# State-space decay factors: the mask by GpSimd, the column's decay as the exponential's bias

## The chip, the cores and the metric

The kernel runs on one core of one Trainium2 chip. The metric is the device time of one execution in microseconds. Before the change it is 2160.16 us, the median of three runs (2158.58 to 2160.63).

## The reference, cut to what matters

A sequence of 256 rows and 1024 columns passes four layers. Each layer is a SwiGLU block, a mixer and a second SwiGLU block, each followed by a layer norm. The mixers of layers 0 and 3 are state-space mixers; those of layers 1 and 2 are two kinds of attention. The part of the state-space mixer that the change touches is this:

```
a_cs     = cumsum(dt * a)                       # per head, along the 256 rows
decay_in = exp(where(l >= s, a_cs[l] - a_cs[s], -inf))
cb       = einsum('bclgn,bcsgn->bcgls', c, b)   # per group of eight heads
m        = cb * decay_in                        # per head, rows l, columns s
y_diag   = einsum('bcgrls,bcsgrp->bclgrp', m, xdt)
```

There are 32 heads in four groups of eight. A head's factor is zero above the diagonal, and it is multiplied by the group's `cb`.

## The kernel before

The 256 rows are two halves of 128, `t` = 0 and 1, which run as two interleaved streams on the same weights; the second follows the first by two pieces of weights (`LAG`). A piece is a tile `raw` of 128 x 2048 numbers. It is loaded by SyncE (SP), split by ScalarE (ACT) into a rounded part `wh` (L123) and by VectorE (DVE) into the rest `wl` (L124), four instructions each, and multiplied three times (L148 to L150: `wh` by `xh`, `wl` by `xh`, `wh` by `xl`). A scheduler orders the instructions of each engine from the program and its own estimate of durations. Each engine then works through its list strictly in order; so does each DMA queue.

In a state-space layer a group `g` goes through these stages in both streams:

- `stage_x` and `stage_bc` copy a finished projection out of its PSUM bank (L445, L453), transpose it on TensorE (PE) and put it in `xb`; `conv` (L423 to L434) runs on ACT and DVE, and the second stream's call does both halves.
- `stage_back` (L459) transposes back, makes `xdt`, `xD` and `xe` on DVE, multiplies b by c on PE (L478), and copies the result to `cb`. The first 128 columns are multiplied by the triangle mask on DVE (L481); the second stream's other 128 columns are copied by ACT (L483).
- `stage_m` (L496), twice per group and stream, makes the factors of four heads in a tile `mt` of 128 x 512. A DMA broadcasts four rows of running sums to all partitions (L500). DVE subtracts the column's sum and caps the difference at zero, one head at a time (L502). ACT takes the exponential of the whole tile (L503), and DVE multiplies it by `cb` (L504). The cap keeps the exponential finite above the diagonal, where the masked `cb` makes the product zero. Five buffers hold `mt`; each is free again when PE's last product with it is done.
- `stage_off` (second stream only) multiplies the carried state by `cb` on PE (L489), scales it (L491) and adds it (L494).
- `stage_y` multiplies each head's factor by `xdt` on PE (L512) and adds on DVE (L514); `stage_z` is the gate out of its PSUM bank (L519).
- `stage_n` multiplies by the gate (L524), squares on ACT (L526), scales the mean on DVE (L527), takes a power of -1/2 on GpSimd (POOL, L528) and scales the row by it on DVE (L529). `stage_a` transposes that on PE (L158) and splits it into `ah` and `al` for the output product.

So a layer has 16 tiles `mt` and eight of the powers. In these layers POOL otherwise does only small fills; its DMAs belong to the SwiGLU blocks.

Of the kernel before, what the change touches and what calls it, by code (L numbers as in the profile page):

```python
# [7 lines left out]
F32 = mybir.dt.float32  # L8
FR = mybir.dt.float32r
BF = mybir.dt.bfloat16  # L10
AF = mybir.ActivationFunctionType
ALU = mybir.AluOpType
# [11 lines left out]
NEG = -1e30  # L24
# [25 lines left out]
def build(tc, x, wst, ln_g, ln_b, sm_dt, sm_rows, sm_conv, sm_nw, fx_f, fx_b, out, plan=None):  # L50
    nc = tc.nc
    ctx = ExitStack()
    cpool = ctx.enter_context(tc.tile_pool(name="const", bufs=1))
# [13 lines left out]
    def T():  # L67
        return ps_t.tile([128, 512], F32, name="tp")
# [7 lines left out]
    def tmp(cols, tag, bufs, dt=F32):  # L76
        return spool.tile([128, cols], dt, name=tag, tag=tag, bufs=bufs)
# [6 lines left out]
    K = {}  # L84

    def consts():
        if K:
            return
        up = tmp(128, "t1", 5)
        make_upper_triangular(nc, up, val=1.0, diag=True)  # L90
        lo = tmp(128, "t1", 5)
        make_lower_triangular(nc, lo, val=1.0, diag=False)
        K["tri"] = cpool.tile([128, 128], FR, name="tri")
        nc.vector.tensor_copy(K["tri"], up)
        K["ntri"] = cpool.tile([128, 128], FR, name="ntri")
        nc.vector.tensor_scalar_mul(K["ntri"], up, -1.0)
        K["sel"] = cpool.tile([128, 32], FR, name="sel")
        nc.vector.tensor_add(K["sel"], ident[:, 0:32], ident[:, 32:64])
        K["strict"] = cpool.tile([128, 128], FR, name="strict")
        nc.vector.tensor_copy(K["strict"], lo)  # L100
        K["idb"] = cpool.tile([128, 128], BF, name="idb")
        nc.vector.tensor_copy(K["idb"], ident)
        K["mlo"] = cpool.tile([128, 128], BF, name="mlo")
        nc.vector.tensor_scalar_mul(K["mlo"], lo, NEG)
        K["mup"] = cpool.tile([128, 128], BF, name="mup")
        nc.vector.tensor_sub(up, up, ident)
        nc.vector.tensor_scalar_mul(K["mup"], up, NEG)
# [251 lines left out]
    def ssm_small(j):  # L359
        if j in ssms:  # L360
            return ssms[j]
        consts()
        s = St()
        s.dt = small_w(sm_dt[j], 32)
        s.rows = tmp(96, "rows", 1)
        nc.sync.dma_start(s.rows, bc(sm_rows[j:j + 1, :], 96))
        s.conv = spool.tile([128, 24, 5], F32, name="conv", bufs=1)
        nc.sync.dma_start(s.conv, sm_conv[j])
        s.na = tmp(32, "na", 1)
        nc.scalar.activation(s.na, s.rows[:, 32:64], AF.Exp)  # L370
        nc.vector.tensor_scalar_mul(s.na, s.na, -1.0)
        s.nw = {}
        s.xb, s.cv, s.B, s.xe = {}, {}, {}, {}
        ssms[j] = s
        return s
# [7 lines left out]
    def ssm(st, j):  # L383
        t = st.t
        s = ssm_small(j)
        d = St()
# [72 lines left out]
        def stage_back(g):  # L459
            cv = s.cv[g]  # L460
            h8 = slice(g * 8, g * 8 + 8)
            tp = T()
            for k in range(4):
                nc.tensor.transpose(tp[:, k * 128:(k + 1) * 128], cv[:, k, mine], ident)
            tp8 = tp.rearrange("p (a b) -> p a b", a=8)

            def times(tag, rows, bufs):
                o = tmp(512, tag, bufs)
                nc.vector.tensor_mul(o.rearrange("p (a b) -> p a b", a=8), tp8,
                                     rows[:, h8].unsqueeze(2).to_broadcast([128, 8, 64]))  # L470
                return o
            xds[g] = (times(f"xdt{t}", d.dt, 1 + t), times("xD", s.rows[:, 64:96], 2))
            if t == 0:
                s.xe[g] = times("xe", d.de, 1)
            tp = T()
            for n in range(1 + t):
                B = cv[:, 4, mine if n == 0 else slice(0, 128)]
                nc.tensor.matmul(tp[:, n * 128:(n + 1) * 128], B, cv[:, 5, mine], start=True, stop=True)  # L478
            cb = tmp(256, "t1", 5)
            nn = (1 + t) * 128  # L480
            nc.vector.tensor_mul(cb[:, :128], tp[:, :128], K["tri"].bitcast(F32))  # L481
            if t:
                nc.scalar.activation(cb[:, 128:], tp[:, 128:256], AF.Copy)  # L483
            cbs[g] = cb
            mts[g] = []

# [9 lines left out]
        def stage_m(g, qd):  # L496
            e = spool.tile([128, 4, 128], F32, name="mt", bufs=5)
            h0 = g * 8 + qd * 4
            row = d.cum[h0:h0 + 4, :].rearrange("h l -> (h l)").unsqueeze(0)
            nc.sync.dma_start(e.rearrange("p a b -> p (a b)"), row.to_broadcast([128, 512]))  # L500
            for h in range(4):
                nc.vector.tensor_scalar(e[:, h], e[:, h], d.ncum[:, h0 + h:h0 + h + 1], 0.0, op0=ALU.add, op1=ALU.min)  # L502
            nc.scalar.activation(e, e, AF.Exp)  # L503
            nc.vector.tensor_mul(e, e, cbs[g][:, 0:128].unsqueeze(1).to_broadcast([128, 4, 128]))  # L504
            mts[g].append(e)

# [37 lines left out]
        for g in range(N_GRP):  # L544
            b = where["X", g, 2]
            at(b - 1, stage_x, g)
            at(b, stage_bc, g)
            c = b + (LAG if t == 0 else 0)
            at(c + 1, stage_back, g)
            at(c + 2, stage_m, g, 0)  # L550
            at(c + 2, stage_m, g, 1)
            if t == 1:
                at(c + 2, stage_off, g)
            z = where["Z", g, 1]
            at(z, stage_z, g)
            iy = c + 3
            at(iy, stage_y, g)
            n = max(iy, z)
            at(n, stage_n, g)
            at(min(n + 1, where["O", g, 0] - 1), stage_a, g)  # L560
# [16 lines left out]
    def fox_small(j):  # L577
        if j in foxs:
            return foxs[j]
        consts()  # L580
        s = St()
        s.f = small_w(fx_f[j], 16)
        s.rows = tmp(16, "rows", 1)
        nc.sync.dma_start(s.rows, bc(fx_b[j:j + 1, :], 16))
        s.kT, s.v = {}, {}
        foxs[j] = s
        return s

    def attn(st, kind, j):
# [3 lines left out]
        if fox:  # L593
            s = fox_small(j)

            def stage_f():
                v = small_proj(st, s.f, 16, s.rows)
                q = log1p_exp(v, 16)
                m = small()
                nc.vector.tensor_scalar_min(m[:, :16], v, 0.0)  # L600
                lf = small()
                nc.vector.scalar_tensor_tensor(lf[:, :16], q[:, :16], -2.0, m[:, :16], op0=ALU.mult, op1=ALU.add)
                d.h, d.l = small_split(lf[:, :16])

            def stage_cum():
                d.rows = rows_T(d.h, d.l, K["ntri"], f"rowsT{t}")
                if t == 0:
                    s.toend = rows_T(d.h, d.l, K["strict"], "rowsTe")
        else:
            key = ("m", j)  # L610
            if key not in foxs:
                consts()
                foxs[key] = St()
                foxs[key].kT, foxs[key].v = {}, {}
            s = foxs[key]
# [315 lines left out]
```

## Time and profile before

| | us |
|---|---|
| median of three runs | 2160.16 |
| the profiled execution, whole | 2158.25 |
| its span | 2156.1 |
| PE busy | 2122.0 |
| DVE busy | 1486.4 |
| ACT busy | 1125.5 |

The granted TensorE clock is 0.999 of full speed over the span. The state-space layers lie at about 190 to 400 us and 1760 to 1970 us. An engine's busy share is counted over all stages, while the two state-space layers are a fifth of the span, so their own stretch has to be looked at. Instructions of one engine overlap by some tenths of a microsecond: a run of equal instructions takes less than their number times the mean of one.

### The profile page before, as it was taken

How to read it: one execution, taken by the hardware profiler on the slowest of the kernel's cores; microseconds unless marked ns; L12 is line 12 of the kernel's file. 1: busy time of each engine (PE TensorE's matmuls, PEld its weight loads, DVE VectorE, ACT ScalarE, POOL GpSimd, SP SyncE). 2: the span in 40 equal slices, each digit the busy share in tenths (PEclk: the TensorE clock that was granted, in tenths of full speed). 3: DMA queues.
4: the chain of work that ended last, by engine and by line, in shares of the span. 5: the costliest groups of instructions: out<-in, count | busy, mean ns of one | idle time of the engine just before them, and what ended most of it. 6: DMA issues, size and time to landing. Idle time of an engine off the chain costs nothing.

```text
span 2156.1 us, 29943 instructions
## 1 busy us (share of the span) xinstructions
PE 2122.0 (98%) x10370; PEld 1768.2 (82%) x10370; DVE 1486.4 (69%) x2959; ACT 1125.5 (52%) x2314; POOL 477.6 (22%) x862
## 2 busy tenths in 40 slices
PE   8999999999999999999999999999999999999998
PEld 6888878788888888888888888888888888788887
DVE  6657999855765674665575574666575679998655
ACT  6444776544444555444544455544454447665442
POOL 2331000233143200043233300033323310001431
PEclk9999999999999999999999999999999999999999
DMA  9775544676586643476666654376767665556772
GB/s 316 229 230 187 191 173 153 225 232 227 193 255 226 218 158 118 137 237 226 220 226 228 226 199 136 131 220 227 226 224 236 221 205 180 162 179 207 235 226 94
DMA packets 225927, 438.81 MB, mean 204 GB/s; under 512 B 20464, under 2 KB 20976, under 8 KB 225776
## 3 DMA queue, kind: packets, MB, share of 16 engines
q1 hardware_dynamic: 197616, 394.92, 55.1%
q0 software_dynamic: 28160, 41.99, 7.0%
q8 instruction: 81, 1.33, 0.3%
q14 instruction: 70, 0.57, 0.1%
HBM read 414.74 MB, written 22.09 MB: 203 GB/s over the span
## 4 chain that ended last, share of the span: by engine, by line
PE 93%; DVE 3%; ACT 1%; DMA 1%; issue 0%; POOL 0%; SPq 0%; DVEq 0%; ACTq 0%
PE gu L148 15%; PE gu L150 15%; PE gu L149 15%; PE acc L150 9%; PE acc L148 9%; PE acc L149 9%; PE ga L150 4%; PE ga L149 4%; PE ga L148 4%; PE tp L158 3%; PE gu L512 1%; DMA raw<-in_w_dram 1%; PE tp L657 1%; DVE wl L124 1%; DVE mt L502 1%
## 5 line engine op out<-in xcount | busy, mean ns | idle before, releaser
L124 DVE TENSOR_TENSOR wl<-raw,wh 128x512 fp32r<-128x512 f32 x1408 | 887.7, 683 | 361.8 <-ACT wh L123 360.2
L123 ACT ACTIVATE wh<-raw 128x512 fp32r<-128x512 f32 x1408 | 777.0, 621 | 528.0 <-PE gu L150 222.4
L148 PE MATMUL gu<-wh,xh 128*128 128x512 f32 (+1 forms) x1600 | 620.6, 388 | 7.1 <-ACT t L519 2.7
L150 PE MATMUL gu<-wh,xl 128*128 128x512 f32 (+1 forms) x1600 | 617.8, 387 | 0.9 <-DVE xl L124 0.9
L149 PE MATMUL gu<-wl,xh 128*128 128x512 f32 (+1 forms) x1600 | 617.4, 386 | 0.0
L246 POOL DMA_DIRECT2D aT<-turn x640 | 348.3, 551 | 503.4 <-issue 301.9
L148 PEld LDWEIGHTS gu<-wh,xh 128*128 128x128 f32 x1600 | 301.1, 188 | 69.7 <-ACT t L519 3.1
L150 PE MATMUL acc<-wh,al 128*128 128x512 f32 x896 | 353.5, 395 | 0.0
L149 PE MATMUL acc<-wl,ah 128*128 128x512 f32 x896 | 352.5, 393 | 0.0
L148 PE MATMUL acc<-wh,ah 128*128 128x512 f32 x896 | 351.5, 393 | 0.0
L150 PEld LDWEIGHTS gu<-wh,xl 128*128 128x128 f32 x1600 | 300.9, 188 | 61.6 <-DVE xl L124 2.1
L149 PEld LDWEIGHTS gu<-wl,xh 128*128 128x128 f32 x1600 | 301.2, 188 | 59.4 <-issue 0.5
L272 DVE TENSOR_TENSOR t<-t,gu 128x256 f32<-128x256 f32 x176 | 73.5, 418 | 192.5 <-ACT t L270 192.5
L270 ACT ACTIVATE t<-gu 128x256 f32<-128x256 f32 x176 | 67.5, 383 | 260.3 <-PE gu L150 239.5
L150 PEld LDWEIGHTS acc<-wh,al 128*128 128x128 f32 x896 | 168.4, 188 | 36.8 <-DVE al L124 1.9
L149 PEld LDWEIGHTS acc<-wl,ah 128*128 128x128 f32 x896 | 168.5, 188 | 34.4 <-issue 1.0
L148 PEld LDWEIGHTS acc<-wh,ah 128*128 128x128 f32 x896 | 168.5, 188 | 33.6
L148 PE MATMUL ga<-wh,xh 128*128 128x512 f32 (+1 forms) x448 | 159.6, 358 | 1.4 <-ACT xh L123 1.4
L242 POOL DMA_DIRECT2D turn<-tb x160 | 90.3, 565 | 318.6 <-DVE tb L240 297.7
L150 PE MATMUL ga<-wh,xl 128*128 128x512 f32 (+1 forms) x448 | 157.0, 351 | 0.1
L149 PE MATMUL ga<-wl,xh 128*128 128x512 f32 (+1 forms) x448 | 156.1, 349 | 0.0
L190 POOL TENSOR_TENSOR rstd<-ve,mhalf 128x1 f32<-128x1 f32 x24 | 22.6, 942 | 369.9 <-DVE ve L188 369.9
(179 smaller groups left out, 1707.0 us busy)
## 6 DMA issues: line engine op xcount, KB each, us to landing
raw<-in_w_dram SPq DMA_DIRECT2D x351, 1024.0 KB, 5.6
turn<-tb POOLq DMA_DIRECT2D x160, 128.0 KB, 3.4
aT<-turn POOLq DMA_DIRECT2D x640, 32.0 KB, 4.1
mt<-cums SPq DMA_DIRECT2D x32, 256.0 KB, 4.9
gb<-in_ln_g_dram SPq DMA_DIRECT2D x12, 512.0 KB, 4.6
gb<-in_ln_b_dram SPq DMA_DIRECT2D x12, 512.0 KB, 6.1
nw<-in_sm_nw_dram SPq DMA_DIRECT2D x8, 256.0 KB, 5.6
h<-in_x_dram SPq DMA_DIRECT2D x4, 256.0 KB, 4.3
```

Source lines behind the costliest of these rows:

```text
L123: a = nc.scalar.activation(wh, raw, AF.Copy)
L124: return a, nc.vector.tensor_sub(wl, raw, wh.bitcast(F32))
L148: nc.tensor.matmul(o, xh, wh, start=start, stop=False)
L149: nc.tensor.matmul(o, xh, wl, start=False, stop=False)
L150: nc.tensor.matmul(o, xl, wh, start=False, stop=stop)
L158: nc.tensor.transpose(tp[:, j * 128:(j + 1) * 128], src[:, j * 128:(j + 1) * 128], ident)
L190: nc.gpsimd.tensor_tensor(rstd, ve, mhalf, op=ALU.pow)
L242: nc.gpsimd.dma_start(dr, b.rearrange("p q k t -> p (q k t)"))
L246: nc.gpsimd.dma_start(aT[32 * q:32 * q + 32].rearrange("p i k t -> p i (k t)"), dv[q])
L270: nc.scalar.activation(sg, gu[:, :256], AF.Silu)
L272: nc.vector.tensor_mul(a, sg, gu[:, 256:])
L502: nc.vector.tensor_scalar(e[:, h], e[:, h], d.ncum[:, h0 + h:h0 + h + 1], 0.0, op0=ALU.add, op1=ALU.min)
```

## The change

`stage_back` now copies `cb` whole, 128 columns in the first stream and 256 in the second, on DVE and without the triangle. In `stage_m` a new instruction of POOL adds a mask of zero and -1e30 to the whole tile of four heads after its DMA; ACT then takes the exponential of one head at a time, with the negative of the column's sum as its bias, so that DVE's four subtractions are gone. Above the diagonal the exponential is now zero itself. A constant `mlf` holds the mask.

```diff
@@ consts
+        K["mlf"] = cpool.tile([128, 128], F32, name="mlf")
+        nc.vector.tensor_scalar_mul(K["mlf"], lo, NEG)
@@ stage_back
-            nc.vector.tensor_mul(cb[:, :128], tp[:, :128], K["tri"].bitcast(F32))
-            if t:
-                nc.scalar.activation(cb[:, 128:], tp[:, 128:256], AF.Copy)
+            nc.vector.tensor_copy(cb[:, :nn], tp[:, :nn])
@@ stage_m
             nc.sync.dma_start(e.rearrange("p a b -> p (a b)"), row.to_broadcast([128, 512]))
+            nc.gpsimd.tensor_tensor(e, e, K["mlf"].unsqueeze(1).to_broadcast([128, 4, 128]), op=ALU.add)
             for h in range(4):
-                nc.vector.tensor_scalar(e[:, h], e[:, h], d.ncum[:, h0 + h:h0 + h + 1], 0.0, op0=ALU.add, op1=ALU.min)
-            nc.scalar.activation(e, e, AF.Exp)
+                nc.scalar.activation(e[:, h], e[:, h], AF.Exp, bias=d.ncum[:, h0 + h:h0 + h + 1])
             nc.vector.tensor_mul(e, e, cbs[g][:, 0:128].unsqueeze(1).to_broadcast([128, 4, 128]))
```

The new kernel's lines are numbered a little differently: its addition is L501, its exponential L503, the power still L528, the fill of `xb` L445 (L443 before), `wh` L125 (L123), the copy out of the projection L447 (L445), the activation after the convolution L436 (L434).

On POOL, in the first state-space layer, the fills of `xb` and the powers (`sm` by `mhalf`) of the kernel before stand so:

```order
L443 MEMSET xb 128x6x3
L190 TENSOR_TENSOR rstd<-ve,mhalf 128x1
L443 MEMSET xb 128x6x3
L528 TENSOR_TENSOR sm<-sm,mhalf 128x1 x2
L443 MEMSET xb 128x6x3
L528 TENSOR_TENSOR sm<-sm,mhalf 128x1 x2
L443 MEMSET xb 128x6x3
L528 TENSOR_TENSOR sm<-sm,mhalf 128x1 x2
```

In the changed kernel the 16 additions to `mt` stand between them:

```order
L445 MEMSET xb 128x6x3
L192 TENSOR_TENSOR rstd<-ve,mhalf 128x1
L501 TENSOR_TENSOR mt<-mt,mlf 128x512 x2
L445 MEMSET xb 128x6x3
L501 TENSOR_TENSOR mt<-mt,mlf 128x512 x7
L528 TENSOR_TENSOR sm<-sm,mhalf 128x1 x2
L445 MEMSET xb 128x6x3
L501 TENSOR_TENSOR mt<-mt,mlf 128x512 x2
L528 TENSOR_TENSOR sm<-sm,mhalf 128x1
L501 TENSOR_TENSOR mt<-mt,mlf 128x512
L528 TENSOR_TENSOR sm<-sm,mhalf 128x1
L501 TENSOR_TENSOR mt<-mt,mlf 128x512
```

Nine additions now stand ahead of the first group's two powers. The ninth tile reuses the buffer of the first group's fourth.

On ACT, around the first group's factors in the first layer, the kernel before has one load of the exponential's table ahead of four exponentials (`mt`), between copies of weights (`wh`):

```order
L445 ACTIVATE t_2326<-ga 128x512
L434 ACT_TABLE_LOAD
L434 ACTIVATE cv<-cv 128x512
L123 ACTIVATE wh<-raw 128x512 x4
L483 ACTIVATE t_2280<-tp 128x128
L503 ACT_TABLE_LOAD
L503 ACTIVATE mt<-mt 128x512 x3
L123 ACTIVATE wh<-raw 128x512
L503 ACTIVATE mt<-mt 128x512
L519 ACT_TABLE_LOAD
L519 ACTIVATE t_2368<-ga 128x512
```

In the changed kernel single exponentials stand apart from the rest:

```order
L125 ACTIVATE wh<-raw 128x512 x4
L503 ACTIVATE mt<-mt,ncum 128x128
L436 ACT_TABLE_LOAD
L436 ACTIVATE cv<-cv 128x512
L503 ACT_TABLE_LOAD
L503 ACTIVATE mt<-mt,ncum 128x128 x6
L447 ACTIVATE t_2327<-ga 128x512
L503 ACTIVATE mt<-mt,ncum 128x128 x8
L519 ACT_TABLE_LOAD
L519 ACTIVATE t_2369<-ga 128x512
```

A single exponential ahead of the convolution's activation makes ACT load tables more often: the whole list has 52 loads where it had 40, and all twelve lie in the two state-space layers.

## Rows read from the trace of the kernel before

**Rows 1.** Busy time of each engine, share of the span, number of instructions.

```profile
PE 2122.0 (98%) x10370; PEld 1768.2 (82%) x10370; DVE 1486.4 (69%) x2959; ACT 1125.5 (52%) x2314; POOL 477.6 (22%) x862
```

**Rows 2.** Engine totals by stretch: SwiGLU blocks, then the first state-space layer.

```profile
core 0: us, PE busy (x) PEld busy (x) DVE busy (x) ACT busy (x) POOL busy (x), PEclk, DMA share, GB/s
450.00:620.00 170.00, 170.00 (x760) 140.46 (x759) 110.47 (x206) 81.45 (x169) 49.81 (x90) 1.00 0.68 222
200.00:370.00 170.00, 164.60 (x936) 139.74 (x936) 158.07 (x381) 115.67 (x210) 4.78 (x9) 1.00 0.54 183
```

**Rows 3.** What PE waited for: us in total, times, longest.

```profile
PE gu L489 <- ACT t L483: 2.9, 2, 1.4
PE gu L148 <- ACT t L519: 2.7, 2, 1.4
PE gu L512 <- DVE t L491: 2.1, 2, 1.0
```

**Rows 4.** DVE in order of time at the second group: start, duration, line.

```profile
278.82 3.22 DVE L502 TENSOR_SCALAR mt<-mt,ncum 128x128 f32<-128x128 f32 x16
281.96 2.49 DVE L504 TENSOR_TENSOR mt<-mt,t 128x512 f32<-128x512 f32 x4
```

**Rows 5.** ACT's groups by line and shape: busy us, mean ns.

```profile
L503 ACT ACTIVATE mt<-mt 128x512 f32<-128x512 f32 x32 | 19.5, 627 | 8.3 <-DVE mt L502 7.8
L503 ACT ACT_TABLE_LOAD x12 | 15.4, 1283 | 0.2
L667 ACT ACTIVATE mt<-tp,rs 128x128 f32<-128x128 f32 x32 | 11.3, 365 | 17.1 <-DVE rs L662 17.1
L483 ACT ACTIVATE t<-tp 128x128 f32<-128x128 f32 x8 | 2.2, 272 | 3.9 <-DVE t L481 3.9
```

**Rows 6.** POOL's groups by line: a fill and a select.

```profile
L618 POOL MEMSET qz<- 128x512 f32 x4 | 2.1, 527 | 154.2 <-PE tp L657 120.6 <-DVE t L514 33.6
masks.py:66 POOL TENSOR_SCALAR_AFFINE_SELECT t<-t 128x128 f32<-128x128 f32 x1 | 0.3, 305 | 0.0
```

**Rows 7.** In order of time: the first group's first power and its transposes.

```profile
252.41 0.68 DVE L524 TENSOR_TENSOR t<-t,t 128x512 f32<-128x512 f32 x1
252.58 0.93 POOL L528 TENSOR_TENSOR sm<-sm,mhalf 128x1 f32<-128x1 f32 x1 [18.12 <-DVE sm L527]
254.56 0.60 PE L158 MATMUL tp<-ident,t 128*128 128x128 f32 x4
```

**Rows 8.** The fourth `mt` DMA before that power, on SP's queue, and its landing.

```profile
L500 SPq DMA_DIRECT2D mt<-cums x1: 319/319/319, 248.7 to 248.7; - x1
...
DMA to landing us min/median/max: 4.0/4.0/4.0
```

**Rows 9.** The second group's second power.

```profile
295.79 0.42 DVE L124 TENSOR_TENSOR al<-tp,ah 128x256 fp32r<-128x256 f32 x1
295.95 0.55 POOL L528 TENSOR_TENSOR sm<-sm,mhalf 128x1 f32<-128x1 f32 x1 [2.74 <-DVE sm L527]
```

**Rows 10.** The two `mt` DMAs before that power, and their landing.

```profile
L500 SPq DMA_DIRECT2D mt<-cums x2: 319/320/320, 290.6 to 291.5; - x2
...
DMA to landing us min/median/max: 7.1/7.2/7.4
```

**Rows 11.** The third group's second power, in order of time.

```profile
344.19 0.55 POOL L528 TENSOR_TENSOR sm<-sm,mhalf 128x1 f32<-128x1 f32 x1 [4.70 <-DVE sm L527]
```

**Rows 12.** The `mt` DMA before that power, and its landing.

```profile
L500 SPq DMA_DIRECT2D mt<-cums x1: 319/319/319, 340.1 to 340.1; - x1
...
DMA to landing us min/median/max: 3.4/3.4/3.4
```

**Rows 13.** ACT in order of time ahead of a table load.

```profile
301.34 1.14 ACT L123 ACTIVATE wh<-raw 128x512 fp32r<-128x512 f32 x2
302.49 1.28 ACT L503 ACT_TABLE_LOAD   x1
```

## The prediction

> **What bounds the kernel now.** I read the page's totals first. PE is busy 98% of the span, DVE 69%, ACT 52% [rows 1], so a microsecond counts only where PE waits. The totals by stretch come next. Among the SwiGLU blocks PE has no idle time: 760 matmuls in 170 us, 0.224 us each. In the same length of a state-space layer PE is idle 5.4 us (170 less 164.60), DVE works 158.07 us and ACT 115.67 us [rows 2]. DVE is the engine closest to full there, with 12 us left; ACT has 54 us left and POOL 165. The table of PE's waits names what ends the idle time: the copy of `cb` on ACT, the gate's copy out of its bank on ACT, and the scaling of the carried state on DVE, each once in either layer, 1.0 to 1.4 us [rows 3]. So the change plays for about 5 us a layer on the good side. PE obeys its order, so new waits have no such limit.
>
> **The change part by part**, for one layer; there are two.
>
> *DVE loses work.* 64 subtractions go. Sixteen take 3.22 us [rows 4], 0.20 each in a run, so 12.9 us go. The copies of `cb` stay on DVE at about their old number and cost; I count nothing for them. The sixteen of the second group lie straight ahead of the scaling for which PE waits, with four multiplications behind them [rows 4]. Their place is taken by exponentials that ACT can do while DVE is still at the weights, so this wait of 1.0 us [rows 3] should go. I take -1.0. The copy for which the carried product waits (1.4 us) moves from ACT to DVE. It no longer has ACT's hop behind DVE's, but DVE gets to it at the same place in its list: -0.1.
>
> *POOL gains 16 additions of 128x512.* No row shows one. A fill of that shape, without an input, takes 0.53 us, and a select of 128x128, with one input, 0.30 us, four times which is 1.2 us [rows 6]. The lower end is 0.5; the upper end is twice 1.2, for two inputs, 2.4. I take 1.2, the row with an input. The Trainium skill ("GPSIMD Engine Reference", Elementwise — side-by-side cycle accounting) gives 2.6 cycles per element for a two-input addition, an estimate of 1.1 us for 512 elements before its fixed part.
>
> POOL has the time, so what counts is what stands behind an addition in its list. That is the power L528, on which the scaled row, the transposes and the output product hang. Before, the power waited only for DVE. Now the first group's powers stand behind the ninth addition, whose tile can only be fetched when PE has finished with the first group's last one. In the trace that fetch went out at 248.7 and landed 4.0 us later [rows 8]. 252.7 plus 1.2 is 253.9, and the power started at 252.58 [rows 7]: 1.3 us late. PE's order has 25 large matmuls and two small transposes between the group's last product and the transposes in either kernel, and PE came to those transposes without a wait (the row has no bracket) [rows 7]. So 1.3 us stand on PE. At the second group the second power stands behind one addition whose tile was fetched at 290.6 and landed after 7.1 us [rows 10]; 297.7 plus 1.2 is 298.9, against 295.95 [rows 9], 2.9 us late. Here the new order of PE has 16 large matmuls where the old one has 5, besides 24 half-size ones in both; eleven at 0.224 cover 2.5 us. 0.4 us remain. At the third group the fetch at 340.1, 3.4 us and 1.2 us make 344.7 [rows 12] against 344.19 [rows 11], 0.5 us late with one matmul more to cover it: 0.3. The fourth group's powers have no such addition ahead. Sum +2.0. With additions of 0.5 and 2.4 us this is +0.3 and about +5.
>
> *POOL and DVE get into each other's way.* A power of one column took 0.55 us where DVE was at an instruction with one input in PSUM [rows 9], and 0.93 us where DVE had just begun one with both inputs in SBUF, which ran till 253.09 [rows 7]. Something in the power waited for DVE; that an addition holds up DVE in turn, no row shows. If it does for its whole 1.2 us, and three DVE instructions in four have two SBUF inputs (`wl`, the convolution, the products), DVE loses 16 x 1.2 x 0.75 = 14.4 us, as much as it was given. The ends are a loss of 0 and of 29 us (2.4 each). I take the 14.4, since the reverse is seen: DVE's load stays at about 158 us, and nothing is given or taken on PE for it beyond the 1.1 above.
>
> The Trainium skill ("SBUF — State Buffer", Who interferes with whom) says so as a rule: DVE and GpSimd share a pair of ports, a DVE instruction with two SBUF inputs and a GpSimd instruction that reads SBUF exclude each other, and whichever comes second is blocked for the whole of the first. The two powers agree with it. By that rule the change moves DVE's work to a place where DVE pays for it again.
>
> *ACT gains work.* The nearest row to a one-head exponential with a bias is that of the attention's, 0.365 us [rows 5]. Instructions in a run overlap by 0.1 (two copies of weights take 1.14 [rows 13], where an exponential of the same shape shows 0.627 [rows 5]), so 0.27 in a run. 64 x 0.27 is 17.3 us; 16 whole-tile exponentials of 0.627 less 0.1 go, -8.4; six table loads of 1.283 come [rows 5], +7.7; four copies of 0.272 go, -1.1. ACT's list grows by 15.5 us to 131 of 170. The split weights, which are most of ACT's work, are named in none of PE's long waits [rows 3], so I take it that most of this is hidden by their being made ahead; without that cover all 15.5 us would stand on PE, which is the upper end, and 0 is the lower. On the path lie the copies out of PSUM banks that PE wants again: it waited 1.4 us a layer for the gate's [rows 3]. Of the six loads I let one (1.3 us) fall ahead of such a copy, with 0.2 for an exponential that waits for POOL: +1.5.
>
> The Trainium skill ("ScalarE: Activation LUTs", What ACT_TABLE_LOAD costs) counts about 1.38 us of drain with every load. In the trace the load starts 0.01 us after the copies ahead of it end [rows 13], so that no such time shows. By the page the term would be +2.9 and the sum 2.8 us higher over both layers.
>
> *The sum.* -1.0 - 0.1 + 2.0 + 1.5 = +2.4 us a layer, +4.8 in all. The profiled execution took 2158.25 us, 2.15 us more than its span, so 2163.0. The runs' median is 1.9 us above that execution, which would make it 2165. I say 2164.
>
> **The rivals.**
>
> *DVE's relief lasts (faster).* One mechanism: the additions don't hold DVE up, and DVE's 12.9 us let it run ahead of PE. Then the waits on DVE and on ACT behind DVE go, at most the 5.4 us a layer. For it: DVE has only 12 us left in the stretch, and the wait on L491 lies behind the removed work. Against it: the power's 0.93, and POOL's list. With two thirds of the idle time gone and 2 us of late powers hidden by the earlier start, -3.5 a layer: 2153. It decides if an addition costs DVE under 0.4 us.
>
> *The waits trade places (same).* The late powers and the vanished waits cancel, and ACT's loads hide in its 54 us. For it: all terms are 1 to 2 us. Time: 2160, within 3 us.
>
> *The port makes DVE the bound (slower by more).* By the port rule, as a mechanism here: additions of 2.4 us block DVE for 29 us a layer; 158 - 13 + 29 is 174 us in a stretch of 170. PE then waits for `wl`, 4 us a layer, and the late powers grow to 5 us, less the 1.0 that goes: +8 a layer, 2175. For it the two powers; against it that DVE instructions from PSUM can go on meanwhile, and that no row has an addition so long.
>
> **How the numbers follow.** No change can be told within 0.2%, 4.3 us. My forecast, slower by 1 to 11 us, has 0.46 (0.30 slower by over 0.2%, 0.16 within). DVE's relief has 0.24 (0.20 faster, 0.04 within), the trade 0.18 (0.13 within, 0.05 faster), the port as the bound 0.12 (all slower). That makes faster 0.25, same 0.33, slower 0.42. The range runs from 2152, just past the relief's 2153, to 2178, past the 2175 of the port; beyond it lie the longer tails of ACT's cost. The forecast's own range is 2159 to 2171.
>
> **What the changed profile would show.** If the steps are right: PE waits at the first group's transposes for DVE's L529, which waits for POOL, whose power starts right behind an addition; the wait of L512 on L491 is gone; POOL's additions take about 1.2 us; DVE instructions with two SBUF inputs are longer beside them; ACT has 52 table loads. The forecast is wrong if the power still waits for DVE alone, if DVE's instructions keep 0.68 us beside an addition, or if PE's waits in the layer fall under 3 us.

## The result, and the profile after

The changed kernel takes 2178.66 us (median of 5 runs, 2176.69 to 2179.07) against 2160.26 for the kernel before in the same session: a ratio of 1.0083 [1.0072, 1.0094], some 18 us slower. The profiled execution has a span of 2175.0 us against 2156.1, and its mean granted clock is 0.995 against 0.999.

The same stretch of the state-space layer, by its totals (span start, length, busy time and count of each engine, then the granted clock):

```profile
200.00:370.00 170.00, 158.58 (x878) 133.51 (x878) 147.57 (x300) 122.31 (x243) 29.20 (x25) 0.97 0.49 173
```

PE has done 878 matmuls where it had done 936 [rows 2]. DVE is busy for 147.57 us, less than the 158.07 of before: it is not full. The stretch also holds less of the layer now; for each matmul of PE, DVE is busy as long as before (0.168 us against 0.169). The clock, 1.00 before, is 0.97. So PE is late for things that DVE, with 22 us of idle time, makes too late.

What PE waited for over the whole program (us in total, times, longest), the answer to [rows 3]:

```profile
PE tp L160 <- DVE t L529: 7.3, 6, 2.6
...
PE tp L160 <- DVE t L455: 3.5, 1, 3.5
...
PE tp L403 <- ACT dah L125: 3.3, 2, 1.6
PE gu L150 <- DVE t L514: 2.2, 2, 1.1
...
PE gu L150 <- ACT t L519: 1.2, 2, 0.6
PE gu L512 <- DVE mt L504: 1.1, 1, 1.1
PE gu L512 <- DVE t L491: 0.9, 1, 0.9
...
PE gu L489 <- DVE t L483: 0.7, 2, 0.3
```

The three waits of [rows 3] have all shrunk: the copy of `cb` from 2.9 us to 0.7 (now on DVE), the gate's copy from 2.7 to 1.2, the scaling of the carried state from 2.1 to 0.9. Grown or new, among others, are the scaled row (L529), the copy of B and C out of their bank (L455), the step widths (`dah`) and the group's sum (L514). Three of the four are made by DVE, and the fourth by ACT, which had waited for DVE, as follows.

The first place in order of time (start, duration, engine, line; in brackets the idle time before it and what ended it):

```profile
221.03 2.86 POOL L501 TENSOR_TENSOR mt<-mt,mlf 128x512 f32<-128x512 f32 x2 [22.38 <-DMA mt<-cums]
221.07 1.29 DVE L316 TENSOR_SCALAR sm<-sm 128x32 f32<-128x32 f32 x1
...
222.67 1.28 DVE L318 SCALAR_TENSOR_TENSOR sm<-sm 128x32 f32<-128x32 f32 x1
...
224.27 0.18 DVE L318 SCALAR_TENSOR_TENSOR sm<-sm 128x32 f32<-128x32 f32 x1
...
224.88 0.63 ACT L436 ACTIVATE cv<-cv 128x512 f32<-128x512 f32 x1 [1.94 <-DVE cv L433]
...
229.22 0.29 ACT L125 ACTIVATE dah<-sm 128x128 fp32r<-128x128 f32 x1
229.57 0.33 PE L403 MATMUL tp<-tri,dah 128*128 128x128 f32 x1 [1.63 <-ACT dah L125]
```

Two additions run on POOL. Beside each of them one small DVE instruction takes 1.29 or 1.28 us, which takes 0.18 when nothing runs on POOL (the row at 224.27; L316 has a mean of 0.177 in e1, without additions). DVE loses 2.2 us; ACT waits 1.94 of them for the convolution; its list, in which `dah` stands further on, is late by as much; PE waits 1.63.

The costliest place is in the second layer:

```profile
1827.95 2.99 POOL L501 TENSOR_TENSOR mt<-mt,mlf 128x512 f32<-128x512 f32 x2 [2.44 <-DVE xD L494]
1828.39 6.47 DVE L126 TENSOR_TENSOR wl<-raw,wh 128x512 fp32r<-128x512 f32 x4
1831.22 3.08 POOL L501 TENSOR_TENSOR mt<-mt,mlf 128x512 f32<-128x512 f32 x2 [0.28 <-DMA mt<-cums]
...
1835.38 0.41 DVE L455 COPY t<-ga 128x256 f32<-128x256 f32 x1
1835.85 0.69 PE L160 MATMUL tp<-ident,t 128*128 128x128 f32 x2 [3.48 <-DVE t L455]
...
1836.76 0.63 PE L151 MATMUL ga<-wl,xh 128*128 128x512 f32 x1
1837.19 0.63 PE L152 MATMUL ga<-wh,xl 128*128 128x512 f32 x1
...
1842.08 0.39 PE L150 MATMUL ga<-wh,xh 128*128 128x512 f32 x1
1842.31 0.39 PE L151 MATMUL ga<-wl,xh 128*128 128x512 f32 x1
```

Four additions meet four weight splits, which take 6.47 us; three of them take 1.88 where POOL does nothing (the row at 285.00 of e5, below), so four some 2.5. The copy of the bank, behind them in DVE's list, comes 4 us late and PE stands for 3.48. When it goes on, its large matmuls start 0.43 us apart (1836.76, 1837.19) where they later start 0.23 apart. The granted clock of these stretches is the column before the last two:

```profile
1830.00:1835.00 5.00, 2.37 (x11) 1.63 (x9) 5.00 (x4) 1.65 (x4) 4.02 (x3) 1.00 0.22 65
1835.00:1840.00 5.00, 4.15 (x11) 3.38 (x12) 4.38 (x10) 3.02 (x6) 0.93 (x1) 0.50 0.60 211
1840.00:1845.00 5.00, 5.00 (x25) 4.19 (x25) 3.85 (x9) 3.90 (x9) 0.93 (x1) 0.82 0.16 61
```

After a stretch in which PE worked 2.37 of 5 us, the granted clock is 0.50, the 1.2 GHz level, and it is back at 2.4 GHz within the next 5 us. The same follows the wait at 229.57 (0.66 from 230 to 235). It does not follow every such wait: behind those of 1.63 us at 1808.49 and of 2.59 us at 1935.64 the granted clock stays at 1.00. By the mean clock the slow stretches hold at most some 9 us (0.005 of 2175 less 0.001 of 2156). PE's busy time says nearly the same: for the same 10370 matmuls it is 7.0 us longer than before (2129.0 against 2122.0). The other 11.9 us of the longer span are time in which PE stands.

### The profile page after: what moved, and what is told of

Read it like the earlier page. It is cut to its first block, busy times and chain, and to the rows that moved or that the text cites. A ratio compares the mean times of both kernels' runs of the same rounds, so it can differ in the third digit from the quotient of the medians.

```text
span 2175.0 us, 30015 instructions
## 1 busy us (share of the span) xinstructions
PE 2129.0 (98%) x10370; PEld 1772.0 (81%) x10370; DVE 1487.1 (68%) x2832; ACT 1158.0 (53%) x2414; POOL 527.9 (24%) x894
## 5 line engine op out<-in xcount | busy, mean ns | idle before, releaser
L126 DVE TENSOR_TENSOR wl<-raw,wh 128x512 fp32r<-128x512 f32 x1408 | 898.0, 690 | 369.5 <-ACT wh L125 367.6
L125 ACT ACTIVATE wh<-raw 128x512 fp32r<-128x512 f32 x1408 | 776.5, 621 | 520.9 <-PE gu L152 227.4
```

What stands on the lines that cost most here:

```text
L125: a = nc.scalar.activation(wh, raw, AF.Copy)
L126: return a, nc.vector.tensor_sub(wl, raw, wh.bitcast(F32))
```

## The experiments

Theory P was that the additions on POOL cost the time, theory A that ACT's short exponentials and table loads do. Theories B, C and Q then ask what it is about the additions: that they hold DVE up, that the chain through them is late, or that the powers behind them are. Theories L and O ask whether lost DVE time costs the same wherever it is lost.

| kernel | median us | ratio to before | DVE busy us | clock |
|---|---|---|---|---|
| before | 2159 to 2160 | 1 | 1486.4 | 0.999 |
| changed | 2178.66 | 1.0083 [1.0072, 1.0094] | 1487.1 | 0.995 |
| e1 no additions | 2146.35 | 0.9939 [0.9927, 0.9952] | 1462.6 | 0.999 |
| e2 additions alone | 2187.04 | 1.0134 [1.0118, 1.0149] | 1514.8 | 0.995 |
| e3 additions on DVE | 2150.67 | 0.9960 [0.9947, 0.9972] | 1481.6 | 0.999 |
| e4 `cb` whole alone | 2160.81 | 1.0008 [0.9999, 1.0017] | 1487.3 | 0.998 |
| e5 additions beside | 2170.21 | 1.0048 [1.0031, 1.0065] | 1481.7 | 0.992 |
| e6 fills beside | 2147.32 | 0.9943 [0.9928, 0.9958] | 1465.1 | 0.999 |
| e7 powers earlier | 2183.55 | 1.0106 [1.0091, 1.0121] | 1489.2 | 0.994 |
| e8 select on POOL | 2155.42 | 0.9982 [0.9973, 0.9991] | 1471.3 | 0.998 |
| e9 two additions on DVE | 2170.80 | 1.0057 [1.0044, 1.0069] | 1500.2 | 0.993 |
| e10 clamp on ACT | 2150.51 | 0.9960 [0.9946, 0.9973] | 1462.8 | 0.999 |
| e11 `dah` on DVE | 2176.28 | 1.0078 [1.0064, 1.0092] | 1486.9 | 0.993 |

**e1, the changed kernel without the additions.**

```diff
-            nc.gpsimd.tensor_tensor(e, e, K["mlf"]..., op=ALU.add)
...
-            nc.vector.tensor_scalar_mul(d.ncum, ps[:, :32], -1.0)
+            nc.vector.tensor_scalar_mul(d.ncum, ps[:, :32], 1.0)
```

> The changed kernel without its 32 additions on POOL (the triangle mask is left out and the bias of the exponential has its other sign, so that every factor stays finite: the decay factors are not the reference's). The exponentials by head, the whole copy of cb and the DVE without subtractions stay. Theory P (the additions cost the time: they hold up DVE's instructions, and the powers and exponentials stand behind them): no addition, so 2152 to 2162 us, and the waits of PE on L529 and L527 go back to the 0.9 us a layer of before. Theory A (ACT costs the time: 64 short exponentials a layer and their table loads come ahead of copies that PE waits for): the time stays at 2170 to 2180, the wait on the dah copy and the slow clock behind it stay.

2146.35 us: faster than before by 12.6. Theory A falls. ACT has the same 64 short exponentials and table loads a layer as the changed kernel, and of PE's waits in the first layer only three are left (us in total, times, longest):

```profile
PE gu L150 <- ACT t L518: 0.6, 1, 0.6
PE tp L160 <- DVE t L528: 0.5, 2, 0.4
PE gu L489 <- DVE t L483: 0.3, 1, 0.3
```

The rest of the change is a gain, then, and the 32 additions cost 32.3 us, one microsecond each (31.0 if the two kernels before, 2160.26 and 2158.99, are set equal). The time came out below the range of theory P too: I had not expected the relief to be worth so much.

**e2, the kernel before with the additions put in.**

```diff
+            nc.gpsimd.tensor_tensor(e, e, K["mlf"]..., op=ALU.add)
             for h in range(4):
                 nc.vector.tensor_scalar(e[:, h], e[:, h], d.ncum[...], 0.0, op0=ALU.add, op1=ALU.min)
```

> The kernel before, with the 32 additions of the mask on POOL put in ahead of its subtractions; the subtractions, the whole-tile exponentials and the masked cb stay. Theory P: all of the additions' cost and none of the relief, so 2174 to 2190 us, with powers behind additions. Theory A: the additions are hidden by POOL's free time, 2158 to 2166, and PE's waits are those of before.

2187.04 us, 28 more than before, as theory P has it. The waits are those of the changed kernel (same columns), though ACT works as before, and the three of [rows 3] are there too (2.9, 2.8 and 2.1 us):

```profile
PE tp L160 <- DVE t L532: 7.1, 7, 3.2
PE tp L160 <- DVE t L455: 3.9, 2, 2.0
...
PE tp L403 <- ACT dah L125: 3.7, 2, 1.9
```

**e3, the additions on DVE.**

```diff
-            nc.gpsimd.tensor_tensor(e, e, K["mlf"]..., op=ALU.add)
+            nc.vector.tensor_tensor(e, e, K["mlf"]..., op=ALU.add)
```

> The changed kernel with its 32 additions on DVE in place of POOL. DVE then pays about 0.7 us for each, nearly what the four subtractions took (0.8). Theory P: POOL's queue and the hold-up of DVE are gone, so 2156 to 2166 us. Theory A: ACT has the same exponentials and table loads as in the changed kernel, so 2172 to 2182.

2150.67 us, better than either theory's range and than both kernels. DVE does the 32 additions at 0.69 us each (19.0 us more busy time than in e1) for 4.3 us. Of POOL, nearly idle here, and DVE, nearly full, DVE was the better place.

**e4, `cb` copied whole, alone.**

```diff
-            nc.vector.tensor_mul(cb[:, :128], tp[:, :128], K["tri"].bitcast(F32))
-            if t:
-                nc.scalar.activation(cb[:, 128:], tp[:, 128:256], AF.Copy)
+            nc.vector.tensor_copy(cb[:, :nn], tp[:, :nn])
```

> The kernel before with cb copied whole by DVE (the triangle mask is left out, so the products above the diagonal are not the reference's) and nothing else changed. Both theories: PE's wait for the copy on ACT (1.4 us a layer) shrinks to under 0.5; the time is 2157 to 2161 us.

2160.81 us, no change that can be told. The wait did not shrink to 0.5: PE waits 1.3 us for the copy on DVE (line 481 there) where it had waited 1.4 for ACT's. DVE gets to it no earlier, which is what the prediction said of this edit (-0.1).

**e5, additions on POOL that nobody waits for.**

```diff
-            nc.gpsimd.tensor_tensor(e, e, K["mlf"]..., op=ALU.add)
+            junk = spool.tile([128, 4, 120], F32, name="junk", bufs=1)
+            nc.gpsimd.tensor_tensor(junk, cbs[g][:, 0:120]..., K["ntri"]..., op=ALU.add)
```

> The changed kernel without its additions on the tiles mt (mask left out, bias of the other sign: the decay factors are not the reference's), with 32 additions of 128x480 on POOL at the same places of the program that read cb and a constant and write a scratch tile that nobody reads. No exponential waits for them. Theory B (an addition blocks a DVE instruction for about a microsecond, whoever uses its result): most of the 32 us between the changed kernel and the one without additions comes back, 2166 to 2178 us, and DVE's instructions with their inputs in SBUF are longer beside the additions. Theory C (the chain fetch, addition, exponential, product is what is late): 2146 to 2152 us, since nothing of it stands in that chain.

2170.21 us: 23.9 of the 32.3 us come back with additions whose result is not used, and no instruction waits for them in the trace, so theory B holds. The 8.4 us left are no measure of theory C, since these additions also take DVE less time (19.1 us in place of 24.5) and start at other moments. Its chain shows little in the changed kernel: DVE stands for 1.8 us in all for the exponentials (2.1 before), and PE for 1.1 for `mt`. The largest wait of the first layer in order of time:

```profile
275.84 4.47 POOL L500 TENSOR_TENSOR junk<-t,ntri 128x480 f32<-128x480 f32 x3
...
276.24 4.63 DVE L124 TENSOR_TENSOR wl<-raw,wh 128x512 fp32r<-128x512 f32 x3
280.79 2.48 DVE L503 TENSOR_TENSOR mt<-mt,t 128x512 f32<-128x512 f32 x4
283.20 0.68 DVE L489 TENSOR_TENSOR t<-gu,ec 128x512 f32<-128x512 f32 x1
...
283.93 3.67 PE L511 MATMUL gu<-xdt,mt 128*128 128x64 f32 x16 [2.32 <-DVE t L489]
...
285.00 1.88 DVE L124 TENSOR_TENSOR wl<-raw,wh 128x512 fp32r<-128x512 f32 x3
```

Three splits take 4.63 us beside three additions, and 1.88 when POOL is done. The 2.7 us lost there are the 2.32 for which PE waits. The waits are the smaller part of the cost: over the whole program PE stands 9.0 us longer than in e1, and is busy 17.0 us longer with the same matmuls. Behind this wait the granted clock is 0.50:

```profile
285.00:290.00 5.00, 5.00 (x19) 4.49 (x19) 2.57 (x5) 0.00 (x0) 0.00 (x0) 0.50 0.40 130
```

**e6, fills in place of those additions.**

```diff
+            nc.vector.tensor_copy(junk[:, 0, 0:1], cbs[g][:, 0:1])
+            for _ in range(3):
+                nc.gpsimd.memset(junk, 0.0)
```

> As the run with the additions beside, but with three fills of 128x480 on POOL in place of each addition (about 1.5 us of POOL, no input read; a copy of one column on DVE ties them to the place). Theory B, if it is POOL's reading that holds DVE up: 2146 to 2154 us and DVE's instructions at 0.68. Theory Q (what stands in POOL's list ahead of the powers is late, whatever it does): as with additions beside, 2160 to 2175 us.

2147.32 us, 1.0 above e1. POOL is as busy as in e5 (525.6 and 526.6 us), and DVE's products of two SBUF tiles keep their time (mean ns behind the comma; 954 in the changed kernel):

```profile
L525 DVE TENSOR_TENSOR t<-t,t 128x512 f32<-128x512 f32 x16 | 10.9, 684 | 0.0
```

What holds DVE up is POOL's reading of SBUF, not its being busy. The Trainium skill says so ("SBUF — State Buffer", Who interferes with whom: a DVE instruction with two SBUF inputs contends with a GpSimd instruction that reads SBUF and not with one that only writes it); e5 and e6 agree.

**e7, the powers earlier in POOL's list.**

```diff
+            with tc.high_priority():
                 nc.vector.tensor_mul(y1, y1, th)
...
                 nc.gpsimd.tensor_tensor(ss[:, 2:3], ss[:, 1:2], mhalf, op=ALU.pow)
                 nc.vector.scalar_tensor_tensor(y1, y1, ss[:, 2:3], nw, op0=ALU.mult, op1=ALU.mult)
```

> The changed kernel with the normalisation chain (product, squares, power, scaling) scheduled at high priority, so that most powers stand one to three additions earlier in POOL's list; the additions stay. Theory Q: PE's waits on L529 (4.5 us in the first layer) go, 2164 to 2171 us. Theory B: the additions still block DVE, 2172 to 2182 us.

2183.55 us, no gain. But the edit did little of what it was meant to: in the trace only two of a layer's eight powers stand earlier in POOL's list, by one addition each, and the order of the other engines moved as well. The waits on the scaled row come to 6.7 us (7.3 in the changed kernel) with one of 3.3. So this run says little about theory Q. e5 says more: its waits on the scaled row are 1.0 us, as in e1, and its 23.9 us are there all the same.

**e8, a select with one input on POOL.**

```diff
-            nc.gpsimd.tensor_tensor(e, e, K["mlf"]..., op=ALU.add)
+            nc.gpsimd.affine_select(out=e, in_=e, compare_op=ALU.is_ge, fill=NEG, base=0, pattern=[[0, 4], [1, 128]], channel_multiplier=-1)
```

> The changed kernel with each addition on POOL replaced by a select of 128x512 with one input (it keeps the triangle and fills the rest with the mask's value; the mask tile is not read). Four selects of 128x128 took 1.2 us in the trace of before, so POOL's time is that of the additions. If two inputs on POOL are what blocks DVE: 2150 to 2160 us. If one is enough: 2172 to 2184 us, as the changed kernel.

2155.42 us. The number fits the first answer and the trace does not. I had taken the select to be as long as an addition, and its shortest takes 0.63, an addition's 1.27; beside it DVE is held up all the same, for a shorter time:

```profile
221.42 1.55 POOL L501 TENSOR_SCALAR_AFFINE_SELECT mt<-mt 128x512 f32<-128x512 f32 x2 [22.39 <-DMA mt<-cums]
221.45 0.64 DVE L316 TENSOR_SCALAR sm<-sm 128x32 f32<-128x32 f32 x1
...
222.41 0.61 DVE L318 SCALAR_TENSOR_TENSOR sm<-sm 128x32 f32<-128x32 f32 x1
```

0.64 in place of 1.29 for the same instruction L316. DVE's busy time is 8.7 us above e1's, and the time 9.1. One input on POOL is enough, and DVE is held up for as long as POOL's instruction takes (0.64 beside 0.63, 1.29 beside 1.27).

**e9, two additions on DVE.**

```diff
-            nc.gpsimd.tensor_tensor(e, e, K["mlf"]..., op=ALU.add)
+            nc.vector.tensor_tensor(e, e, K["mlf"]..., op=ALU.add)
+            nc.vector.tensor_tensor(e, e, K["mlf"]..., op=ALU.add)
```

> The changed kernel with each addition on POOL replaced by two on DVE (the mask is added twice; a factor above the diagonal is 0 either way). DVE then spends 2 x 0.69 us on each tile, 44 us in all, more than the about 25 us that the additions on POOL took from it. Theory L (what DVE loses is what counts, wherever it is lost): more than the changed kernel, 2176 to 2195 us. Theory O (the loss costs so much because POOL's additions stop DVE out of its order, in front of instructions that others wait for, while DVE's own additions stand where its list has room): one addition cost 4.3 us over none, so two cost 8 to 12: 2154 to 2160 us.

2170.80 us, between the two theories, and neither holds as it stands. The first 19.0 us of DVE's work cost 4.3 us, the next 18.6 cost 20.1: theory O's straight line is wrong. DVE is busy for 160.66 us of the stretch of 170 here; that its free time is used up is a likely reason, which no run tests alone. Nor is all of it waiting: of the 22.7 us between the spans of e9 and e3, 11.0 are PE's longer busy time. But with 13 us more of busy DVE than the changed kernel this one is 8 us faster, so theory L's equal price is wrong too. The clock fell here as well (0.993 over the span, 0.52 in the 5 us from 400, where PE had waited 2.03 us), with no addition on POOL.

**e10, the clamp on ACT.**

```diff
             for h in range(4):
-                nc.scalar.activation(e[:, h], e[:, h], AF.Exp, bias=d.ncum[...])
+                nc.scalar.activation(e[:, h], e[:, h], AF.Relu, scale=-1.0, bias=d.ncum[...])
+            nc.scalar.activation(e, e, AF.Exp, scale=-1.0)
```

> A version without the mask's addition: the clamp goes to ACT as a Relu by head with scale -1 and the column's decay as its bias, the exponential takes the whole tile with scale -1, and cb keeps its triangle by the product on DVE, with its second half copied by DVE too. No subtractions and no additions on DVE or POOL; ACT has 16 whole-tile exponentials a layer more than the changed kernel, in fewer groups. If ACT has the time (the theory that its exponentials are hidden): 2145 to 2151 us, below the additions on DVE (2150.7). If ACT's list becomes late: 2155 to 2170 us.

2150.51 us, as fast as e3 and within the first range, though not below e3. ACT is busy for 1169.4 us (1156.6 in e1) and still has the time, or nearly: the 4.2 us above e1 are not explained by any run.

**e11, `dah` made by DVE.**

```diff
-              split(v..., h..., l...)
+            nc.vector.tensor_copy(hv, src)
+            nc.vector.tensor_sub(l..., src, hv.bitcast(F32))
```

> The changed kernel, additions on POOL and all, with the copy dah of the step widths made by DVE, next to dal, in place of ACT, where it stands behind a table load and an exponential. In the changed kernel PE waits 1.6 us for it in either layer, and behind the first of these waits 8 large matmuls go at 0.43 us in place of 0.227. Theory W (each wait of PE counts by itself, and the slow clock behind it too): 2 x 1.6 for the waits and 1.6 to 2 for the slow matmuls go, 2172 to 2175 us. Theory U (the wait only shows DVE's delay upstream, two instructions of 1.29 us, and comes out at the next thing DVE makes): 2177 to 2180 us, with the lost wait found again at another line.

2176.28 us, between the two ranges, and the changed kernel's time within both intervals. Theory U is the better one, though not by its line: the wait did not move elsewhere but stayed, for the same matrix from another engine:

```profile
PE tp L160 <- DVE t L533: 15.4, 10, 3.0
...
PE tp L407 <- DVE dah L299: 3.5, 2, 1.8
```

3.5 us where there were 3.3. ACT's table load ahead of `dah` was not its cause. The additions are: e1, without them, has no wait for `dah`; that it is DVE's lost 2.2 us is read from the rows at 221.07 and 222.67. The waits on the scaled row have doubled (7.3 us in the changed kernel) and the time has not grown with them, which stays open.

## Why the prediction was wrong

It said slower and gave 2164; the time is 2178.66, just outside its range (2152 to 2178). That it came out slower is in part luck: the sum was positive by late powers and by ACT's work, which between them hold little of the 18 us. By its steps:

*The wait on L491 goes, -1.0 a layer.* Not in the changed kernel: the product with the factors (L512) waits 1.1 us for `mt` in the first layer and 0.9 for L491 in the second. In e1 and e3 neither stands among the first layer's waits. The step was right about the removed work and wrong about what the additions leave of it.

*The copy of `cb`, -0.1.* Right for the edit alone (e4). In the changed kernel the wait falls from 1.4 to 0.3, and it does so in e1 too, since DVE there reaches the copy earlier.

*POOL's additions take 1.2 us.* Right: the shortest takes 1.27. The mean is longer (mean ns behind the comma); that POOL waits for DVE in its turn would fit, and no run tests it:

```profile
L501 POOL TENSOR_TENSOR mt<-mt,mlf 128x512 f32<-128x512 f32 x32 | 50.0, 1576 | 94.7 <-DMA mt<-cums 91.3 <-DVE xD L494 2.4 <-PE gu L512 0.5
```

*The powers behind additions, +2.0.* In the first layer the first place came as forecast, 1.41 us for 1.3; in the second layer PE does not wait for it. At the second place, 0.4 forecast, POOL had finished the addition 0.70 us before the power, which waited for DVE. At the third, 0.3 forecast, PE waited 2.59:

```profile
257.53 1.76 POOL L501 TENSOR_TENSOR mt<-mt,mlf 128x512 f32<-128x512 f32 x1 [0.38 <-DVE xb L457]
259.25 0.55 POOL L528 TENSOR_TENSOR sm<-sm,mhalf 128x1 f32<-128x1 f32 x1
260.73 0.63 PE L160 MATMUL tp<-ident,t 128*128 128x128 f32 x4 [1.41 <-DVE t L529]
...
347.48 1.77 DVE L126 TENSOR_TENSOR wl<-raw,wh 128x512 fp32r<-128x512 f32 x1
...
350.87 1.78 DVE L524 TENSOR_TENSOR t<-t,t 128x512 f32<-128x512 f32 x1
...
354.33 0.55 POOL L528 TENSOR_TENSOR sm<-sm,mhalf 128x1 f32<-128x1 f32 x1 [2.23 <-DVE sm L527]
355.81 1.06 PE L160 MATMUL tp<-ident,t 128*128 128x128 f32 x8 [2.59 <-DVE t L529]
```

The power at 354.33 waits for DVE, POOL having been idle for 2.23 us. What is late there is the product at 350.87, 1.78 us long, and the splits before it. Worked as the 1.3 was, the ends of this term would be +0.6 and +5.7, not +0.3 and about +5; the forecast does not use them.

*DVE loses 14.4 us a layer to the additions.* Right in size: 24.5 us over both layers between e1 and the changed kernel, 12.3 a layer. And it is as much as was given, as the step said: 1487.1 us of busy time against 1486.4.

*"DVE's load stays at about 158 us, and nothing is given or taken on PE for it beyond the 1.1 above."* This is the step that failed. It took equal amounts of DVE time to be worth the same. What the program lost for each microsecond of DVE's busy time, by the table of runs, and how much longer PE stood in the profiled execution:

| what DVE got | DVE us more | time us more | per us | PE idle us more |
|---|---|---|---|---|
| one addition in its own list (e3 over e1) | 19.0 | 4.3 | 0.23 | 2.9 |
| two (e9 over e1) | 37.6 | 24.5 | 0.65 | 14.6 |
| held up by selects (e8 over e1) | 8.7 | 9.1 | 1.04 | 6.7 |
| held up by unused additions (e5 over e1) | 19.1 | 23.9 | 1.25 | 9.0 |
| held up by the change's (changed over e1) | 24.5 | 32.3 | 1.32 | 21.6 |
| held up, subtractions kept (e2 over before) | 28.4 | 28.1 | 0.99 | 20.3 |

In no row did PE's idle time grow by more than DVE's busy time. A price above 1 holds, besides, the longer busy time of PE behind its waits, where the clock is low: 17.0 us in e5, 9.3 in the changed kernel, 0.8 in e3.

An addition of POOL's starts when its tile lands. It holds up the DVE instruction with inputs in SBUF that comes next then, and two to four come together (6.47 us in place of 2.5 at 1828). DVE's own additions stand at a place of its list that the scheduler chose. That the place is a reason for the higher price fits every run, by PE's idle time too (0.15 and 0.39 for each microsecond in DVE's own list, 0.47 to 0.88 where it is held up), but no run changed the place alone. Nor are the 8.4 us that e5 lacks of the 32.3 (narrower by a sixteenth, with no exponential waiting) divided; the powers' part is small by the trace, since DVE stands for 9.0 us for them where it stood for 6.2 before.

*ACT's work, +1.5.* Failed: e1 has all of it, and its waits on ACT in the first layer are 0.6 us.

Two more amounts were missing, one on either side. The rest of the change is worth 12.6 us, where the prediction gave it 1.1 a layer and a cost of 1.5: in the stretch of 170 us PE is idle for 1.6 us in e1, of the 5.4 of before. The rival in which DVE's relief lasts had seen 7 of the 12.6. And no step had a price for the clock, which falls behind the waits at 229.57, 355.81 and 1835.85; PE is busy 9.3 us longer than in e1 for the same matmuls. Of the rivals, the port as the bound had the blocking and nearly the time (2175), but not the way: additions of 2.4 us were to fill DVE, and DVE is idle for 22 of 170 us.

## What to carry to other kernels

Free time on an engine is no reason to give it work: ask whether its instructions stop another engine's, and on the critical list of which engine. Here 32 elementwise additions on an idle POOL cost 32 us and on a DVE at 93% in that stretch 4. Two rows with one instruction at two lengths (L318, 0.18 and 1.28 us), and what runs on the neighbour then, show it sooner than any total.

## What the hardware showed

- A DVE instruction whose only input is a small SBUF tile (the constant multiplication and addition L316, 128x32) is held up as well, for 1.29 us beside an addition; copies out of PSUM keep their time (L449, a mean of 684 ns against 682 before), and so do products with an input there (`xdt`, 689 against 687); a product of two SBUF tiles goes from 683 to 954 (mean ns behind the comma, changed kernel):

```profile
L316 DVE TENSOR_SCALAR sm<-sm 128x32 f32<-128x32 f32 x4 | 2.9, 736 | 0.1
L449 DVE COPY xb<-tp 128x512 f32<-128x512 f32 x16 | 10.9, 684 | 0.7 <-PE tp L160 0.7
L524 DVE TENSOR_TENSOR t<-t,t 128x512 f32<-128x512 f32 x16 | 15.3, 954 | 0.0
```

- A select of 128x512 on POOL takes 0.63 us at its shortest, half the 1.2 that four times the 128x128 one gave, and a fill of 128x480 takes 0.50; beside 96 of them DVE's products of two SBUF tiles stay at 684 ns.
- In the changed kernel the granted clock was 0.50 for the 5 us behind a wait of PE of 3.5 us, and 1.00 behind waits of 1.63 and 2.59 us in the same layer.
